# A two-layer decoder trunk in float32: last product with tokens in the rows, coefficient loads on GpSimd's queue, eight buffers for u, and fourteen products on ones at the start

## The chip, the core and the metric

The kernel runs on one core of a Trainium2 chip. The metric is device time in microseconds (us) of one execution, median over runs; lower is better. TensorE is written PE (its weight loads PEld), VectorE DVE, ScalarE ACT, GpSimd POOL, and SyncE SP; SP's and POOL's queues issue DMAs.

## What is computed

The input x has 256 tokens of width 4096. Two layers follow each other; `mem` is a fixed memory of 256 tokens, and every weight is float32.

```
for i in range(2):
    hn   = rmsnorm(h, pre_norm[i])
    u, gate, q, q_gate = split(hn @ w_in[i])            # 3072, 3072, 1024, 1024 wide
    y    = s5_mixer(u, ...) if i == 0 else rglru_mixer(u, ...)
    m    = memory_attention(q, rmsnorm(mem, mem_norm[i]), w_kv[i])
    out  = concat([y * silu(gate), m * silu(q_gate)]) @ w_out[i]     # 4096 wide
    h    = h + rmsnorm(out, post_norm[i])
```

`s5_mixer` is a diagonal state-space recurrence with 192 groups of 16 channels and 64 complex states. Its input coefficients (kept in `Bs` on the chip and in `wD` in DRAM) are a product of `b_re`, `b_im` with powers of a discretised decay that is worked out on the chip.

## The kernel before

Every large product is done in float32 precision from two rounded parts: a raw weight tile of 128 x 1024 (512 KB, tile `raw`) is cast by ACT into `hi`, DVE subtracts to get `lo`, and PE adds hi x hi, hi x lo and lo x hi. One raw tile is one **step**; there are 968 such steps and 12 small ones for the recurrent gates. A step streams 6144 columns through PE in every form. The forms differ in what is held in the array. In "n8", "n2", "n4" and "w2" the weights are held and the activations (`A`, `Bhn`, `Bmix`: features in the rows, 256 tokens along the columns) stream past: "w2" needs 8 products of 512 columns and 8 of 256 a step, the "n" forms 24 of 256. In "v" the activations are held, 128 tokens at a time, and the weights stream: 12 products of 512 columns a step, and the result has tokens in the rows.

The program is written out in one pass by `run`: for each step it places what is due (evacuations, loads, pieces of the side work), then PE's products, then the cast two steps ahead; raw loads are placed four to five steps ahead and go through SP's queue in the order of the program, as all of `dma`'s transfers do. `wraw` has 4 buffers, `whi` and `wlo` 6 halves each (three steps).

The places that matter here:

- **The start.** `setup` sets a tile of ones; the first product of phase "u0" waits for x, its scaled part `A` and the first `hi`.
- **Phase "u0" (24 row blocks).** `ev_u0` multiplies each finished block into a tile `e1` of which there are three, and two steps later sends it to DRAM twice: as `uX` in 64 x 4 x 64 pieces and as `uF`.
- **S5's coefficients.** `s5` is a generator of side work on DVE. It stores the decay as `aD` (three DMAs), later copies `in_s5b3` into `wD`, and then for each half of the groups runs `s5_a_b`: a load step (one DMA of `in_s5bc` and eight of `aD` into `Bs`), three steps of waiting, then multiplications of 128 x 768 on DVE with three pairs of stores `wD<-Bs`. Both halves use the same region of `Bs`. All of it goes through SP's queue. After the stores, `x_load` reads `wD` and `uX` back.
- **The last product (phase "out1").** 128 steps in form "w2" with features in the rows. `ev_out1` squares, scales and keeps each block and loads the residual `h1` beside it; after the last one `rstd` sums the squares over the rows with products on ones, and `final` multiplies and adds in nine pieces (four additions on POOL) and stores them, with features in the rows.

Of the kernel before, what the change touches and what calls it, by code (L numbers as in the profile page):

```python
# [11 lines left out]
F32 = mybir.dt.float32  # L12
# [16 lines left out]
L4 = 4  # L29
TQ = T // L4  # L30
MAGIC = 12582912.0
AHEAD = 8

SM = {}
# [12 lines left out]
def blocks(nm, form=None, n=0):  # L47
    return ([(0, n, form)] if form else []) + [(n, nm - n, "w2")]
# [2 lines left out]
FORMS = {"u0": [(0, 8, "n8"), (8, 4, "n2"), (12, KE - 12, "w2")], "g0": blocks(KE), "gq0": blocks(KX), "q0": blocks(KX),  # L51
         "k0": blocks(KX, "n4", 4), "v0": [(0, KX, "v")], "k1": blocks(KX),
         "glu": blocks(KE, "n4", 4), "out0": blocks(KD), "v1": [(0, KX, "v")],
         "u1": blocks(KE), "gq1": blocks(KX), "q1": blocks(KX), "g1": blocks(KE), "out1": blocks(KD)}


def size(ap):
# [6 lines left out]
class Trunk:  # L64
# [69 lines left out]
    def dma(self, out, in_):  # L134
        out, in_ = (a.bitcast(F32) if a.dtype == F32R else a for a in (out, in_))
        self.nc.sync.dma_start(out=out, in_=in_)  # L136

    def fill(self):
        if self.pieces:
            self.pieces.popleft()()  # L140
# [9 lines left out]
    def setup(self):  # L150
        tc, ctx = self.tc, self.ctx
        P = lambda name, bufs, **kw: ctx.enter_context(tc.tile_pool(name=name, bufs=bufs, **kw))
        self.cpool = P("const", 1)
        self.wraw = P("wraw", 4)
        self.whi = P("whi", 6)
        self.wlo = P("wlo", 6)
        self.big = P("big", 1)
        self.ev = P("ev", 3)
        self.stp = P("st", 2)
        self.ps_acc = P("psacc", 4, space=PSUM)  # L160
        self.ps_x = P("psx", 3, space=PSUM)
# [12 lines left out]
        self.h1 = dt("h1", [KD, 128, T])  # L174
        self.qd = [dt(f"qd{i}", [KX, 128, T]) for i in range(2)]
        self.sq = [dt(f"sqd{i}", [KX, 128, T]) for i in range(2)]
        self.kd = [dt(f"kd{i}", [KX, 128, T]) for i in range(2)]
        self.vd = [dt(f"vd{i}", [2, 128, XA]) for i in range(2)]
        c = self.cpool
        self.sm = c.tile([128, SM_W], F32, name="sm")  # L180
        self.ones = c.tile([128, 128], F32, name="ones")
        self.ident = c.tile([128, 128], F32, name="ident")
        self.n4sp = c.tile([128, KE], F32, name="n4sp")
        self.acc = c.tile([128, 2, T], F32, name="acc")
        self.rbx = c.tile([128, T], F32, name="rbx")
        self.rbm = c.tile([128, T], F32, name="rbm")
        self.colm = c.tile([128, 2], F32, name="colm")
        self.nc.vector.memset(self.ones, 1.0)
        make_identity(self.nc, self.ident)

    def small(self, name, i, n=1):
        o = SM[name][0] + i
# [266 lines left out]

    def ev_u0(self, m, ps):  # L460

        u = self.e("e1")
        v = lambda t: t.rearrange("p (t e) -> p e t", e=L4)
        self.mul(u.rearrange("p (e t) -> p e t", e=L4), v(ps), v(self.rbx))

# [164 lines left out]
            self.put_mixed(self.A, m, g)  # L630
        self.at(self.step + 1, b)

    def ev_out1(self, m, accs, i):
        if m == 0:
            self.fin = self.big.tile([128, 2, KD, T], F32, name="Bfin", tag="B")

        def out(k, ps, g):
            self.act(self.fin[:, 0, k, :], ps, AF.Identity, scale=g)
            self.dma(self.fin[:, 1, k, :], self.h1[k])
        self.ev_out(1, m, accs, i, out, lambda: self.rstd(None, self.colm2, self.step, then=self.final))  # L640

    def final(self):
        k0 = 0
        for c, n in enumerate((4, 4, 4, 4, 4, 4, 4, 2, 2)):
            k = slice(k0, k0 + n)
            k0 += n
            rb = self.pm[:, 0, :].unsqueeze(1).to_broadcast([128, n, T])
            o, h = self.fin[:, 0, k, :], self.fin[:, 1, k, :]
            self.mul(o, o, rb)
            if c in (0, 2, 3, 5):  # L650
                self.nc.gpsimd.tensor_tensor(out=o, in0=o, in1=h, op=ALU.add)  # L651
            else:
                self.add(o, o, h)
            q = self.nc.scalar if c % 2 else self.nc.sync
            q.dma_start(out=self.out[k].rearrange("k p t -> p k t"), in_=o)


    def poly(self, p, x, cs):
# [92 lines left out]
    def s5(self):  # L751
# [43 lines left out]
        self.recip(den, den)  # L795
        yield
        for k, n, rows in ((0, 0, asb[0:NT, 0]), (1, 0, asb[NT:128, 0]), (1, 128 - NT, asb[0:2 * NT - 128, 1])):
            self.dma(self.aD[n:n + rows.shape[0], :, k], rows.rearrange("n (g q) -> n g q", g=2))
        self.mul(t0, nr, lr)
        self.mul(t1, ai, li)  # L800
        self.add(t0, t0, t1)
# [26 lines left out]
        self.mul(t0, nr, den)  # L828
        self.ts(A4[:, :, 0, 1], t0, 2.0, ALU.mult)
        self.ts(A4[:, :, 1, 0], t0, -2.0, ALU.mult)  # L830
        self.dma(self.wD[:, :, L4 - 1].rearrange("t g c x -> t g (c x)"), I["s5b3"].rearrange("t g c x -> t g (c x)"))
        yield
        for h in range(2):
            for f in self.s5_a_b(X0[:, 4096:], h * KE // 2, KE // 2):
                yield f() if f else "wait"
        for _ in range(3):
            yield "wait"
        self.nc.gpsimd.memset(X[:, :, :, 0:1], 0.0)
# [147 lines left out]
    def s5_a_b(self, region, t0, n):  # L986
# [6 lines left out]
        bc = lambda k, h: A[:, h, k].unsqueeze(2).to_broadcast([128, n // 2, 2, 64])  # L993

        def load():
            self.dma(B, self.I["s5bc"][:, tt])
            for g in range(2):
                for i in range(4):
                    r = slice(64 * g + i, 64 * g + 64, 4)
                    self.dma(A[r].rearrange("p t k q -> p t (k q)"),  # L1000
                             a5[i, g, tt].unsqueeze(0).to_broadcast([16, n, 128]))

        def store(e, y):
            for g in range(2):
                r = slice(64 * g, 64 * g + 64)
                self.dma(self.wD[tt, g, e].rearrange("t c (i x) -> (c i) t x", i=4),
                         y[r].rearrange("p t k q -> p t (k q)"))
        work = [load, None, None, None]
        for i, (x, y) in enumerate(((B, P), (P, B), (B, P))):
            def add(h, y=y):  # L1010
                self.sub(y[:, h, 0], y[:, h, 0], Q[:, h, 1])
# [3 lines left out]
                work += [lambda h=h, x=x: self.mul(Q[:, h], x[:, h], bc(1, h)),  # L1015
                         lambda h=h, x=x, y=y: self.mul(y[:, h], x[:, h], bc(0, h)), lambda h=h, add=add: add(h)]
            work.append(lambda i=i, y=y: store(2 - i, y))
        return work

    def seqfill(self):  # L1020
        if self.pieces:
# [212 lines left out]
    def build(self):  # L1234
# [49 lines left out]
        for b in range(12):  # L1284
# [1 line left out]
            self.hook(gates[b] - 12, lambda b=b: self.lru_block(b, self.step + 12))  # L1286
        mark["out1"] = len(self.steps)

        self.add_phase("out1", A, self.ev_out1, ks=list(range(KE, KD)) + list(range(KE)), whole=True,
                       ready=lambda kg: ("att", 1) in self.done)  # L1290


# [67 lines left out]
def layout(i):  # L1360
# [14 lines left out]
    for n, w in W.items():  # L1375
# [5 lines left out]
             "d": cols(A["s5_d"]), "bglu": cols(A["s5_b_glu"]), "cw": cols(A["lru_conv_w"]),  # L1381
             "cb": cols(A["lru_conv_b"]), "ba": cols(A["lru_b_a"]), "bx": cols(A["lru_b_x"]),
             "lam": cols(A["lru_lam"])}
    r["small"] = np.concatenate([parts[n] for n in SM], axis=1)
    pl = lambda v: v.reshape(NT, 128).T
    ls = np.repeat(A["s5_log_step"][0][:, None], 64, axis=1)
# [18 lines left out]
def build_nc(arrays):  # L1405
# [3 lines left out]
    I = {}  # L1409
    for name, a in arrays.items():  # L1410
        I[name] = nc.dram_tensor(f"in_{name}", a.shape, mybir.dt.from_np(a.dtype), kind="ExternalInput").ap()
    out = nc.dram_tensor("out_0", (KD, 128, T), F32, kind="ExternalOutput").ap()
    with tile.TileContext(nc) as tc:
        kernel(tc, I, out)
    return nc
# [10 lines left out]
```

## Time and profile before

| what | us |
|---|---|
| median of 3 runs | 2939.95 (2938.41 to 2943.11) |
| the profiled execution, its own time | 2940.36 |
| its span, first to last instruction | 2938.5 |
| PE busy | 2879.9 (98% of the span) |
| DVE busy / ACT busy / POOL busy | 1994.2 / 1614.4 / 201.1 |
| mean granted clock of PE | 0.994 of 2.4 GHz |

The profiled execution takes 1.9 us more than its span; sums below are made against 2940.36. PE's busy time is modelled from starts, so it counts slow products as busy too: a loss shows either as idle time or as a longer distance from one product to the next.

### The profile page before, as it was taken

The numbers are of one execution on the slowest core, as the hardware profiler recorded it, in microseconds if no ns is written. First come the engines' busy times: TensorE is split into PE (matmuls) and PEld (weight loads), VectorE is DVE, ScalarE is ACT, GpSimd is POOL, SyncE is SP. The second block draws the span as 40 slices with busy tenths as digits, with TensorE's granted clock in tenths as the row PEclk, the third lists the DMA queues.
The fourth block names the chain that finished last, engine by engine and source line by source line (L and its number), as shares of the span: only waits on it lengthen the run. The fifth ranks groups of instructions, "written<-read, shape, count | busy, mean of one in ns | idle before, by whom it ended". The sixth has DMA issues, their size and how long they took to land.

```text
span 2938.5 us, 52696 instructions
## 1 busy us (share of the span) xinstructions
PE 2879.9 (98%) x19182; PEld 2531.3 (86%) x19182; DVE 1994.2 (68%) x3559; ACT 1614.4 (55%) x3042; POOL 201.1 (7%) x223
## 2 busy tenths in 40 slices
PE   8989999999999999999999999999999999999996
PEld 8978888888888898888888888888888888888885
DVE  8776459987695556666555776578888766655555
ACT  6434554445575556566555564466666655555553
POOL 0000000046650000000000110000000000000001
PEclk9999999999999999999999999999999999999998
DMA  8688766676676776676666996666666676666664
GB/s 256 202 257 262 230 198 189 192 218 195 209 217 203 232 242 225 213 242 216 211 199 198 284 293 198 203 207 218 208 217 218 191 225 198 200 203 200 205 202 148
DMA packets 279316, 633.61 MB, mean 216 GB/s; under 512 B 42464, under 2 KB 149216, under 8 KB 279008
## 3 DMA queue, kind: packets, MB, share of 16 engines
q1 hardware_dynamic: 272848, 624.22, 68.2%
q0 software_dynamic: 4352, 4.20, 0.9%
q8 instruction: 150, 2.46, 0.3%
q10 hardware_dynamic: 1856, 1.84, 0.2%
q14 instruction: 110, 0.90, 0.1%
HBM read 585.47 MB, written 46.24 MB: 215 GB/s over the span
## 4 chain that ended last, share of the span: by engine, by line
PE 93%; DVE 3%; DMA 2%; issue 1%; ACT 1%; SPq 0%; DVEq 0%; ACTq 0%
PE acc L132 88%; PE pm L132 2%; PE psg L132 1%; DVE lo L92 1%; PE psx L132 1%; DVE Bs L92 1%; DVE Bfin L92 0%; PE pss L132 0%; PE pso L132 0%; SPq L136 0%; DVE e L92 0%; DMA uF<-e 0%; ACT hi L128 0%; DMA Bs<-in_s5bc 0%; DMA raw<-in_w_u 0%
## 5 line engine op out<-in xcount | busy, mean ns | idle before, releaser
L92 DVE TENSOR_TENSOR lo<-raw,hi 128x512 fp32r<-128x512 f32 x1960 | 1328.3, 699 | 830.0 <-ACT hi L128 812.7
L128 ACT CAST hi<-raw 128x512 fp32r<-128x512 f32 x1960 | 1167.7, 619 | 729.4 <-PE acc L132 607.7
L132 PE MATMUL acc<-A,hi 128*128 128x512 f32 (+1 forms) x4768 | 1478.7, 369 | 9.8 <-ACT A L124 8.0
L132 PE MATMUL acc<-A,lo 128*128 128x256 f32 x4160 | 1168.9, 281 | 17.6 <-DVE lo L92 17.0
L132 PEld LDWEIGHTS acc<-A,hi 128*128 128x128 f32 x4768 | 859.9, 190 | 171.7 <-ACT A L124 8.0
L132 PEld LDWEIGHTS acc<-A,lo 128*128 128x128 f32 x4160 | 788.5, 190 | 24.1 <-DVE lo L92 22.8
L132 PE MATMUL acc<-Bhn,hi 128*128 128x512 f32 x2048 | 719.2, 396 | 2.0 <-ACT hi L128 2.0
L132 PE MATMUL acc<-Bhn,lo 128*128 128x256 f32 x2048 | 572.9, 280 | 1.3 <-DVE lo L92 1.3
L132 PEld LDWEIGHTS acc<-Bhn,hi 128*128 128x128 f32 x2048 | 384.6, 188 | 91.9 <-ACT hi L128 3.1
L132 PEld LDWEIGHTS acc<-Bhn,lo 128*128 128x128 f32 x2048 | 386.6, 189 | 2.8 <-DVE lo L92 2.6
L132 PE MATMUL acc<-Bmix,hi 128*128 128x512 f32 x1024 | 355.0, 394 | 0.0
L132 PE MATMUL acc<-Bmix,lo 128*128 128x256 f32 x1024 | 283.6, 277 | 0.0
L132 PEld LDWEIGHTS acc<-Bmix,hi 128*128 128x128 f32 x1024 | 192.0, 188 | 44.6
L132 PEld LDWEIGHTS acc<-Bmix,lo 128*128 128x128 f32 x1024 | 192.3, 188 | 0.0
L132 PE MATMUL acc<-hi,A 128*128 128x512 f32 x512 | 157.9, 389 | 0.0
L128 ACT COPY e<-acc 128x256 f32<-128x256 f32 x212 | 78.3, 369 | 109.4 <-PE acc L132 108.2
L132 PEld LDWEIGHTS acc<-hi,A 128*128 128x128 f32 x512 | 95.8, 188 | 19.9
L124 ACT ACTIVATE e<-e 128x256 f32<-128x256 f32 x64 | 26.8, 418 | 156.1 <-DVE e L92 155.8
L132 PE MATMUL acc<-lo,A 128*128 128x512 f32 x256 | 99.6, 389 | 0.0
L651 POOL TENSOR_TENSOR Bfin<-Bfin 128x1024 f32<-128x1024 f32 x4 | 10.3, 2588 | 1185.3 <-DVE Bfin L92 1185.3
L92 DVE TENSOR_TENSOR Bs<-Bs 128x256 f32<-128x256 f32 (+3 forms) x131 | 76.3, 586 | 21.8 <-DMA Bs<-aD 21.2
L92 DVE TENSOR_TENSOR e<-e,acc 128x256 f32<-128x256 f32 x212 | 84.5, 411 | 7.1 <-ACT e L128 7.1
(152 smaller groups left out, 1627.9 us busy)
## 6 DMA issues: line engine op xcount, KB each, us to landing
raw<-in_w_out SPq DMA_DIRECT2D x256, 512.0 KB, 4.3
raw<-in_w_u SPq DMA_DIRECT2D x192, 512.0 KB, 4.3
raw<-in_w_g SPq DMA_DIRECT2D x192, 512.0 KB, 4.1
raw<-in_w_glu SPq DMA_DIRECT2D x72, 512.0 KB, 4.3
raw<-in_w_gq SPq DMA_DIRECT2D x64, 512.0 KB, 4.4
raw<-in_w_q SPq DMA_DIRECT2D x64, 512.0 KB, 4.3
raw<-in_w_k SPq DMA_DIRECT2D x64, 512.0 KB, 4.5
raw<-in_w_v SPq DMA_DIRECT2D x64, 512.0 KB, 4.6
```

Source lines behind the costliest of these rows:

```text
L92: self.nc.vector.tensor_tensor(out=out, in0=a, in1=b, op=op)
L124: self.nc.scalar.activation(out=out, in_=a, func=f, **kw)
L128: self.nc.scalar.copy(out=out, in_=a)
L132: self.nc.tensor.matmul(out, lhsT=lhsT, rhs=rhs, start=start, stop=stop)
L651: self.nc.gpsimd.tensor_tensor(out=o, in0=o, in1=h, op=ALU.add)
```

## The change

The phase "out1" takes form "v": 128 tokens are held at a time and the weights stream, so the result has tokens in the rows. Its scale (`post_norm`) is read as rows from a new input `postr`, squares are summed along the free axis by ACT, and `final` turns the residual with PE transposes, scales and adds in 16 pieces on DVE, and stores each. Four kinds of DMA of `s5` (aD, in_s5bc, in_s5b3, wD) go from SP's queue to POOL's by `gdma`; the loads of both halves are issued at once, ahead of most of the decay's powers, into two regions, and the three steps of waiting stand once. `ev_u0` rotates through tags e1, e2, e3 with 3, 3 and 2 buffers. Fourteen products of ones by ones stand at PE's head. The output array and its host layout change to tokens in rows.

```diff
+NWARM = 14
...
-         "u1": blocks(KE), "gq1": blocks(KX), "q1": blocks(KX), "g1": blocks(KE), "out1": blocks(KD)}
+         "u1": blocks(KE), "gq1": blocks(KX), "q1": blocks(KX), "g1": blocks(KE), "out1": [(0, KD, "v")]}
...
+    def gdma(self, out, in_):
+
+        self.nc.gpsimd.dma_start(out=out, in_=in_)
...
+        for _ in range(NWARM):
+            self.nc.tensor.matmul(self.pm[:, 0, 0:128], lhsT=self.ones, rhs=self.ones, start=True, stop=True)
...
     def ev_u0(self, m, ps):
 
-        u = self.e("e1")
+        u = self.ev.tile([128, T], F32, name="u", tag=f"e{m % 3 + 1}", bufs=(3, 3, 2)[m % 3])
...
-    def ev_out1(self, m, accs, i):
...
+    def out1_load(self, g):
+
+        if g == 0:
+            fin = self.big.tile([128, 4, 2048 * 2], F32, name="Bfin", tag="B")
+            self.fo = fin[:, 0:2]
+            self.fh = fin[:, 2:4].rearrange("p a (k t) -> p (a k) t", t=T)
+            self.ssq = self.stp.tile([128, 2, 8], F32, name="nv", tag="nv", bufs=2)
+        self.gain = self.stp.tile([128, 2, T], F32, name="st", tag="st").rearrange("p a b -> p (a b)")
+        self.dma(self.gain, self.I["postr"][g].unsqueeze(0).to_broadcast([128, 512]))
+        for k in range(4 * g, 4 * g + 4):
+            self.dma(self.fh[:, k], self.h1[k])
+
+    def ev_out1(self, g, n, ps):
+        self.mul(self.fo[:, n, 512 * g:512 * g + 512], ps, self.gain)
+        sq = self.stp.tile([128, 2, T], F32, name="sq", tag="sq", bufs=1).rearrange("p a b -> p (a b)")
+        self.act(sq, ps, AF.Square, accum_out=self.ssq[:, n, g:g + 1])
+        if g == 7 and n == 1:
+            self.final()
 
     def final(self):
-        k0 = 0
...
+        pieces = [(n, g) for g in range(8) for n in range(2)]
+        ps = {}
+
+        def turn(i):
+            if i >= len(pieces):
+                return
+            n, g = pieces[i]
+            ps[i] = (self.ps_x if i % 7 < 3 else self.ps_acc).tile([128, 2, T], F32, name="pst" if i % 7 < 3 else "acc",
+                                                                 tag="x" if i % 7 < 3 else "acc")
+            p = ps[i].rearrange("p a b -> p (a b)")
+            for k in range(4):
+                self.nc.tensor.transpose(p[:, 128 * k:128 * k + 128], self.fh[:, 4 * g + k, n * 128:n * 128 + 128],
+                                         self.ident)
+        for i in range(7):
+            turn(i)
+        v = self.stp.tile([128, 2, 8], F32, name="nv", tag="nv", bufs=2).rearrange("p a b -> p (a b)")
+        self.nc.vector.tensor_reduce(out=v[:, 8:10], in_=self.ssq, axis=mybir.AxisListType.X, op=ALU.add)
...
+        for i, (n, g) in enumerate(pieces):
+            o = self.fo[:, n, 512 * g:512 * g + 512]
+            self.stt(o, o, v[:, 4 + n:5 + n], ps.pop(i).rearrange("p a b -> p (a b)"), ALU.mult, ALU.add)
+            q = self.nc.scalar if i % 2 else self.nc.sync
+            q.dma_start(out=self.out[n, :, 512 * g:512 * g + 512], in_=o)
+            turn(i + 7)
...
         for k, n, rows in ((0, 0, asb[0:NT, 0]), (1, 0, asb[NT:128, 0]), (1, 128 - NT, asb[0:2 * NT - 128, 1])):
-            self.dma(self.aD[n:n + rows.shape[0], :, k], rows.rearrange("n (g q) -> n g q", g=2))
+            self.gdma(self.aD[n:n + rows.shape[0], :, k], rows.rearrange("n (g q) -> n g q", g=2))
+        ab = [self.s5_a_b(X0[:, 4096 + 6144 * h:], h * KE // 2, KE // 2) for h in range(2)]
+        for load, _ in ab:
+            load()
...
-        self.dma(self.wD[:, :, L4 - 1].rearrange("t g c x -> t g (c x)"), I["s5b3"].rearrange("t g c x -> t g (c x)"))
-        yield
-        for h in range(2):
-            for f in self.s5_a_b(X0[:, 4096:], h * KE // 2, KE // 2):
-                yield f() if f else "wait"
+        self.gdma(self.wD[:, :, L4 - 1].rearrange("t g c x -> t g (c x)"), I["s5b3"].rearrange("t g c x -> t g (c x)"))
+        yield
+        for _ in range(3):
+            yield "wait"
+        for _, work in ab:
+            for f in work:
+                yield f()
...
-        self.add_phase("out1", A, self.ev_out1, ks=list(range(KE, KD)) + list(range(KE)), whole=True,
+        for g in range(8):
+            self.hook(mark["out1"] + 4 + 16 * g, lambda g=g: self.out1_load(g))
+        self.add_phase("out1", A, self.ev_out1, ks=list(range(KE, KD)) + list(range(KE)),
```

The first place is SP's queue in phase "u0", where the coefficients of the first half are loaded (`raw` is a weight tile, `e_...` and `u` are finished blocks of u, `Bs_370` is the region of the coefficients). Before:

```order
L136 DMA raw<-in_w_u 128x1024
L136 DMA wD<-in_s5b 48x8192
L136 DMA raw<-in_w_u 128x1024
L136 DMA uX<-e_1883 64x4x64 x2
L136 DMA uF<-e_1883 128x256
L136 DMA uX<-e_1885 64x4x64 x2
L136 DMA uF<-e_1885 128x256
L136 DMA Bs_370<-in_s5bc 128x1536
L136 DMA Bs_370<-aD 16x12x128 x8
L136 DMA raw<-in_w_u 128x1024 x6
```

The same place in the changed program:

```order
L137 DMA raw<-in_w_u 128x1024 x2
L137 DMA uX<-u 64x4x64 x2
L137 DMA uF<-u 128x256
L137 DMA uX<-u 64x4x64 x2
L137 DMA uF<-u 128x256
L137 DMA raw<-in_w_u 128x1024 x8
```

The ten coefficient DMAs no longer stand between two raw loads. They stand on POOL's queue, which had none of them (there, row `MEMSET` followed `AFFINE_SELECT` at once); in the changed program POOL's queue begins, behind the identity matrix, with:

```order
L141 DMA aD<-Bs_384 192x1x64
L141 DMA aD<-Bs_384 64x1x64
L141 DMA aD<-Bs_384 128x1x64
L141 DMA Bs_384<-in_s5bc 128x1536
L141 DMA Bs_384<-aD 16x12x128 x8
L141 DMA Bs_384<-in_s5bc 128x1536
L141 DMA Bs_384<-aD 16x12x128 x8
L141 DMA wD<-in_s5b 48x8192
L141 DMA wD<-Bs_384 64x12x128 x12
L879 MEMSET Bs_384 128x192
```

All 34 DMAs of the coefficients stand one behind the other, and the loads of both halves stand ahead of the copy of `in_s5b3` and of every store.

The second place is PE's end, behind the last product. Before (`A` is the mixed activation, `pm` the sums over the rows):

```order
L132 MATMUL acc<-A,lo 128x256
L132 MATMUL acc<-A,hi 128x512
L132 MATMUL acc<-A,lo 128x256
L132 MATMUL pm<-ones,acc 128x1 x4
L132 MATMUL pm<-dg,ones 128x128 x2
```

In the changed program (`Bfin` here is the residual, `pst` and `acc` are the PSUM tiles that take its transposes):

```order
L133 MATMUL acc<-hi,A 128x512 x2
L133 MATMUL acc<-lo,A 128x512
L673 MATMUL pst<-ident,Bfin 128x128 x12
L673 MATMUL acc<-ident,Bfin 128x128 x16
L673 MATMUL pst<-ident,Bfin 128x128 x12
L673 MATMUL acc<-ident,Bfin 128x128 x16
L673 MATMUL pst<-ident,Bfin 128x128 x8
```

The six products of the norm are gone from PE's end, and 64 transposes of the residual stand there.

## Rows read from the trace of the kernel before

**Rows 1.** The page, busy time: engine, us (share), instructions.

```profile
PE 2879.9 (98%) x19182; PEld 2531.3 (86%) x19182; DVE 1994.2 (68%) x3559; ACT 1614.4 (55%) x3042; POOL 201.1 (7%) x223
```

**Rows 2.** Table by stretch: busy us, PE's clock, DMA share, GB/s.

```profile
104.00:141.00 37.00, 34.40 (x277) 33.27 (x276) 27.93 (x77) 14.33 (x25) 0.00 (x0) 1.00 0.70 198
141.00:165.60 24.60, 15.40 (x118) 15.20 (x117) 10.44 (x17) 5.47 (x10) 0.00 (x0) 0.86 0.79 261
205.20:212.90 7.70, 4.64 (x19) 3.74 (x18) 7.27 (x11) 2.90 (x5) 0.00 (x0) 0.78 0.86 282
212.90:260.00 47.10, 47.10 (x268) 40.83 (x268) 38.34 (x62) 21.68 (x37) 2.22 (x3) 1.00 0.97 291
104.00:260.00 156.00, 141.13 (x899) 127.41 (x898) 114.49 (x214) 60.44 (x103) 2.22 (x3) 0.97 0.86 258
2910.80:2938.50 27.70, 2.42 (x14) 1.89 (x12) 20.21 (x24) 2.00 (x5) 10.28 (x4) 0.59 0.46 151
```

**Rows 3.** Timeline of the start: start, length, instruction, [idle before <-releaser].

```profile
0.84 0.17 DVE L188 MEMSET ones<- 128x128 f32 x1 [0.84 <-PEq L1408]
...
7.99 1.10 PE L132 MATMUL acc<-A,hi 128*128 128x256 f32 x2 [7.99 <-ACT A L124]
...
13.58 0.63 PE L132 MATMUL acc<-A,hi 128*128 128x256 f32 x2
...
14.22 0.45 PE L132 MATMUL acc<-A,hi 128*128 128x256 f32 x2
...
15.34 0.40 PE L132 MATMUL acc<-A,hi 128*128 128x256 f32 x2
...
15.70 0.40 PE L132 MATMUL acc<-A,hi 128*128 128x256 f32 x2
```

**Rows 4.** Waits of DVE and PE, 100 to 215 us: total, times, longest.

```profile
DVE e L92 <- DMA uF<-e: 7.7, 4, 5.4
...
PE acc L132 <- DVE lo L92: 14.1, 5, 9.2
```

**Rows 5.** Timeline of DVE where it waits for the coefficients of a half.

```profile
158.53 2.42 DVE L92 TENSOR_TENSOR Bs<-Bs 128x768 f32<-128x768 f32 x3 [13.74 <-DMA Bs<-aD]
...
205.56 2.42 DVE L92 TENSOR_TENSOR Bs<-Bs 128x768 f32<-128x768 f32 x3 [7.44 <-DMA Bs<-aD]
```

**Rows 6.** Timeline of SP's queue, where the first half's coefficients are loaded.

```profile
149.70 5.12 SPq L136 DMA_DIRECT2D Bs<-aD  x8
154.91 13.14 SPq L136 DMA_DIRECT2D raw<-in_w_u  x6
```

**Rows 7.** Timeline of ACT: the copy that the `aD` stores read.

```profile
108.79 0.41 ACT L128 COPY Bs<-psa 128x128 f32<-128x128 f32 x2
```

**Rows 8.** DMA issues: xcount, KB each, median us to landing.

```profile
bh<-in_x POOLq DMA_DIRECT2D x16, 256.0 KB, 7.3
```

**Rows 9.** POOL's one kind of DMA, line 580: ns min/median/max.

```profile
L580 POOL DMA_DIRECT2D bh<-in_x x16: 1194/1203/1332, 1633.8 to 1734.6; - x16
```

**Rows 10.** The chain that ended last, from the last product on: start, us.

```profile
2481.07 429.88 PE acc L132 x2480
...
2914.33 0.17 DVE nv L112
...
2916.09 1.23 PE pm L132 x4
2917.35 2.36 DVE Bfin L92 x2
...
2934.47 0.69 DVE Bfin L92
```

**Rows 11.** Timeline of PE in phase "v1", form "v".

```profile
1759.59 0.62 PE L132 MATMUL acc<-hi,A 128*128 128x512 f32 x2
...
1764.35 0.62 PE L132 MATMUL acc<-hi,A 128*128 128x512 f32 x2
```

**Rows 12.** PE's transposes in the attention: ns min/median/max.

```profile
L1084 PE MATMUL pst<-ident,p x32: 270/272/274, 1075.7 to 2470.6; 128*128 128x128 f32 x32
```

More of the change, by code (lines that the diff above doesn't have):

```diff
@@ L631, in ev_g1 @@
         self.at(self.step + 1, b)
-    def ev_out1(self, m, accs, i):
[L634 to L640, printed above, removed]
-    def final(self):
-        k0 = 0
[L644 to L655, printed above, removed]
+    def out1_load(self, g):
[8 more added lines that the diff above has]
+            self.dma(self.fh[:, k], self.h1[k])
@@ new lines, in ev_out1 @@
+    def ev_out1(self, g, n, ps):
[4 more added lines that the diff above has]
+            self.final()
+    def final(self):
+        pieces = [(n, g) for g in range(8) for n in range(2)]
[14 more added lines that the diff above has]
+        self.nc.vector.tensor_reduce(out=v[:, 8:10], in_=self.ssq, axis=mybir.AxisListType.X, op=ALU.add)
+        self.ts(v[:, 0:2], v[:, 8:10], 1.0 / D, ALU.mult, EPS, ALU.add)
+        self.act(v[:, 2:4], v[:, 0:2], AF.Sqrt)
+        self.recip(v[:, 4:6], v[:, 2:4])
+        self.mul(v[:, 6:8], v[:, 4:6], v[:, 4:6])
+        self.mul(v[:, 6:8], v[:, 6:8], v[:, 0:2])
+        self.ts(v[:, 6:8], v[:, 6:8], -0.5, ALU.mult, 1.5, ALU.add)
+        self.mul(v[:, 4:6], v[:, 4:6], v[:, 6:8])
+        for i, (n, g) in enumerate(pieces):
[4 more added lines that the diff above has]
+            turn(i + 7)
@@ L995, in load @@
         def load():
-            self.dma(B, self.I["s5bc"][:, tt])
+            self.gdma(B, self.I["s5bc"][:, tt])
             for g in range(2):
@@ L999, in load @@
                     r = slice(64 * g + i, 64 * g + 64, 4)
-                    self.dma(A[r].rearrange("p t k q -> p t (k q)"),
+                    self.gdma(A[r].rearrange("p t k q -> p t (k q)"),
                              a5[i, g, tt].unsqueeze(0).to_broadcast([16, n, 128]))
@@ L1005, in store @@
                 r = slice(64 * g, 64 * g + 64)
-                self.dma(self.wD[tt, g, e].rearrange("t c (i x) -> (c i) t x", i=4),
+                self.gdma(self.wD[tt, g, e].rearrange("t c (i x) -> (c i) t x", i=4),
                          y[r].rearrange("p t k q -> p t (k q)"))
-        work = [load, None, None, None]
+        work = []
         for i, (x, y) in enumerate(((B, P), (P, B), (B, P))):
@@ L1017, in s5_a_b @@
             work.append(lambda i=i, y=y: store(2 - i, y))
-        return work
+        return load, work
     def seqfill(self):
@@ L1383, in layout @@
              "lam": cols(A["lru_lam"])}
+    r["postr"] = np.ascontiguousarray(A["post_norm"][1].reshape(8, 512))
     r["small"] = np.concatenate([parts[n] for n in SM], axis=1)
@@ L1411, in build_nc @@
         I[name] = nc.dram_tensor(f"in_{name}", a.shape, mybir.dt.from_np(a.dtype), kind="ExternalInput").ap()
[L1412 removed]
+    out = nc.dram_tensor("out_0", (2, 128, D), F32, kind="ExternalOutput").ap()
     with tile.TileContext(nc) as tc:
@@ L1424 @@
     o = np.asarray(r.results[0]["out_0"])
-    return np.ascontiguousarray(o.reshape(D, T).T).reshape(1, T, D)
+    return np.ascontiguousarray(o.reshape(1, T, D))
```

## Prediction

> **What bounds the kernel.** I read the busy times first: PE is busy 98% of the span [rows 1]. But a busy PE can be a slow one, so the next view is the distance from one product to the next, stretch by stretch. In the last product 2480 products take 429.88 us, 0.1733 each, 2.773 us for a step of 16 [rows 10]; nothing waits there, PE alone sets the time. The losses are at four other places. At the start the first product begins at 7.99 us, and three products of 256 columns take 0.64 us (13.58 to 14.22) until 14.22 and 0.36 after it (15.34 to 15.70): the lower level of the clock, then the upper [rows 3]. From 100 to 215 us PE waits 14.1 us for `lo` tiles of DVE, and DVE waits 7.7 us for the stores of `uF` that keep a u tile occupied [rows 4] and 13.74 and 7.44 us for `aD` loads [rows 5]. What stands behind the waiting instruction in DVE's order are the `lo` tiles of the next steps. At the end nothing but 27.7 us of evacuation, norm and stores is left, with PE busy for 2.4 of it [rows 2]. The stretch between 260 us and the last product is left as it is.
>
> **Products on ones.** Fourteen are added, behind a tile of ones that is written by 1.01 us [rows 3]. Two such products (four instructions) take 1.23 us at the lower level with their latency [rows 10], so fourteen take at most 8.6 us and would end at 9.6, and about half at the upper level, 4.3. So they end between 5.3 and 9.6; back to back, where the latency is paid once, I estimate 7: in time for the first product. If the clock is up by then, the 6.23 us from 7.99 to 14.22 shrink from 9.7 triples of 0.64 to 9.7 of 0.36, 3.5 us: 2.7 gained. If they end at 9.6, 1.6 of that is lost; if the clock is not up, nothing is gained. I take 2.0, nearer the upper end, because 7 us is longer than the 6.23 us after which the clock rose in this trace. The Trainium skill ("TensorE: Matmul & The Clock Gate", Part 1) says that the throttled clock is the default, that activity lifts it, and that the moment does not hang on the kernel's own start but varies from run to run. The trace agrees on the first two (0.64, then 0.36 a triple); one execution cannot show the third, by which this term could be anything from 0 to 2.7.
>
> **u's buffers and the coefficient loads.** What PE lost is taken by pitch. A product of 256 columns costs 0.12 (0.36/3) at the upper level; from 104 to 141 us, 277 of them need 33.2 us and took 37.0: 3.8 lost. From 141 to 165.6, 118 need 14.2 of 24.6: 10.4 lost, one wait of DVE for `aD` and the clock's fall behind it (0.86 granted). From 205.2 to 212.9, 19 products at 0.176 (47.10/268, the next stretch) need 3.3 of 7.7: 4.4 lost to the second half's load and a granted 0.78 [rows 2]. Together 18.6.
>
> With eight tiles instead of three, u's products no longer wait for the stores. With the loads on POOL, SP does not spend 5.12 us on eight of them ahead of six raw loads [rows 6]. Each costs POOL 1.2 us [rows 9], and POOL has nothing else to do there. Are they in time? The copy that `aD` is stored from ends at 109.2 [rows 7]. Three stores (3.6), their landing, nine loads (10.8) and a landing follow: 29 us with the 7.3 that POOL's loads take to land [rows 8]; the second half needs 11 more. DVE stood ready for the first half at 144.8 (158.53 less 13.74 [rows 5]) and will be, with the 3.8 us gained ahead of it, at 141: 31.8 us after the copy. So it fits with 3 us to spare. The second half is asked for a half's work later: from 158.5 to 198.1 (205.56 less 7.44) less three waiting steps of 2.83 (16 products of 0.176), 31 us; it fits with 23 to spare. What hides the whole cost is POOL's idleness and this distance; if it were gone, each late microsecond beyond PE's lead of about two steps (5.5 us) is lost.
>
> What is late next are the raw loads themselves. From 104 to 260 us the DMA engines are used to 0.86 at 258 GB/s, 40.2 MB; 18.6 us less would be 293 GB/s at 0.98. The densest stretch, 212.9 to 260, ran at 291 and 0.97 with no idle PE; the one before it reached 282 [rows 2]. 40.2 MB at 291 leave 0.8 us of the loss standing, at 282 they leave 5.2. The loads now also bunch in the part where u's small pieces are written, so I take 4 back. The step: 18.6 - 4 = 14.6.
>
> **The last product.** Form "v" streams the same columns in 12 products instead of 16. In phase "v1" 21 products take 4.76 us (1759.59 to 1764.35), 2.72 a step of 12 [rows 11]. 128 steps of 2.773 - 2.720 save 6.8 us. Its evacuation (two multiplications on DVE and two squares on ACT per 16 steps) is less than that of before, and DVE and ACT have more than half a step free; "v1" shows the pitch with its evacuation, so I take no other cost.
>
> **The end.** Before, the end takes 27.7 us [rows 2]. Now, behind the last product: one multiplication and one square, which I put at 1.4; a small reduction, 0.2; then the small operations of the norm, 1.5 of the 1.76 between 2914.33 and 2916.09. The copies, additions and the six products go. So the first of 16 pieces starts at 3.1 us. A piece of 512 columns costs DVE between 0.59 (half of 2.36/2) and 0.69 [rows 10]: the last ends at 12.5 to 14.1, and with the 3.3 us that lay behind DVE's last operation before (2935.2 to 2938.5) the end is at 15.8 to 17.4. But the output is 4.19 MB; at 291 GB/s [rows 2] its stores take 14.4 us behind the first piece (3.7), 18.1, and a little for the last landing. The transposes, 64 at no more than 0.27 [rows 12], take at most 17.3, with the last piece and its store 21.3. I take 18.8, the stores: 27.7 - 18.8 = 8.9 saved, between 6.4 and 11.9.
>
> **Sum.** 2.0 + 14.6 + 6.8 + 8.9 = 32.3. The profiled execution took 2940.4 us, 0.4 above the median of the runs; 2940.4 - 32.3 = 2908.
>
> **Rivals.**
> First: the transfers are the bound, and moving them only moves the wait. For it speaks the share of 0.97 to 0.98 that the sum above needs, against it that PE did not idle once at 0.97 [rows 2]. Then DVE or ACT wait for `aD` or raw tiles about as long as now, and of the change 2.0 + 6.8 + 8.9 = 17.7 are left: 2922.7. The Trainium skill ("DMA: Bandwidth & Descriptors", Issuing engines are not separate DMA queues) speaks for this rival: whichever engine issues, the same 16 DMA engines do the work, and only the time to issue is saved. By that rule alone the edit saves SP's 5.12 us twice and no more. The trace shows the sharing only as far as raw loads and coefficients lie in one queue there.
>
> Second, the other side: slower. POOL makes its transfers slowly where they are cut small. A `wD` store has 64 x 12 = 768 runs, the `bh` loads of 1.2 us have 256; by runs a store would cost 3.6 us. A pair's tile is written again one multiplication later, some 10 us (a third of the 31 us of a half's work), and the first load back from `wD` stands on SP ahead of raw loads. Two stores and a landing of 7.3 must fit in that and PE's lead of 5.5: up to about 4.4 us a store nothing is lost; beyond it 6 us per microsecond of store (two of a pair, at two rewritings and one load back). The 32 gained elsewhere are gone, and 6 more, at about 11 us a store, three times the price by runs: 2946 or more.
>
> Third: the end is not shortened. If the transposes, at the lower clock that the end shows (0.59 [rows 2]), do not keep ahead of DVE, or stores of 2 KB rows go slower, 8.9 is lost: 2917. Against it: seven pieces are turned before the first is needed.
>
> **Chances and range.** Forecast 0.62; the first rival 0.18, the third 0.10, the second 0.05; 0.05 for smaller mixtures of the first and the second, 2924 to 2940. Likeliest alone: 2901 to 2914. The range goes from 2897 (start 2.7, nothing taken back, the end at 15.8) to 2924, with the first and the third rival in it. 0.2% (5.9 us) is about what a measurement of this kernel tells from no change: faster 0.92, same 0.03, slower 0.05.
>
> **What would show it.** Start: 0.36 a triple from the first product. u and coefficients: no wait of DVE for `uF`; none for `aD`, and PE idle under 4 us from 104 to 260, with a granted clock of 1.00; raw loads with nothing between them in SP's queue. Last product: 2.72 a step. End: 16 pieces on DVE at 0.6 to 0.7 and stores that reach 290 GB/s. Wrong would be the sum if DVE waits for a load from POOL, if SP's first read of `wD` holds raw loads, or if PE's transposes come late at the end.

## The result, and the profile after

The changed kernel takes 2906.64 us (median of 4 runs, 2902.31 to 2908.03); the kernel before took 2940.09 beside it (2938.41 to 2943.11). The ratio is 0.9886, with a 95% interval of 0.9874 to 0.9897: 33.5 us faster. The profiled execution took 2907.16 with a span of 2905.4, so its span is 33.1 shorter. The forecast was 2908, in a range of 2897 to 2924.

The page's busy times (engine, us, share, instructions) show no more than that the same work is done in less time:

```profile
PE 2880.1 (99%) x18750; PEld 2517.1 (87%) x18750; DVE 1980.9 (68%) x3528; ACT 1596.1 (55%) x2994; POOL 212.3 (7%) x253
```

The table by stretch of the changed kernel (busy us of PE, PEld, DVE, ACT, POOL with their instructions, then PE's clock, the DMA share and GB/s), stretches of [rows 2], then the end, and one about the late raw loads:

```profile
104.00:141.00 37.00, 34.33 (x282) 33.69 (x281) 25.82 (x70) 12.13 (x22) 12.31 (x22) 1.00 0.98 303
141.00:165.60 24.60, 24.60 (x162) 23.00 (x162) 23.03 (x37) 11.91 (x20) 1.56 (x2) 0.93 0.88 285
205.20:212.90 7.70, 7.70 (x46) 6.66 (x45) 7.38 (x12) 3.11 (x5) 0.00 (x0) 1.00 0.94 314
104.00:260.00 156.00, 153.32 (x1051) 138.26 (x1050) 119.71 (x220) 69.18 (x120) 23.60 (x37) 0.99 0.88 278
2887.60:2905.40 17.80, 9.12 (x65) 6.75 (x63) 12.67 (x25) 1.58 (x5) 0.00 (x0) 0.84 0.64 236
110.00:145.00 35.00, 32.33 (x253) 31.69 (x253) 23.03 (x62) 11.82 (x21) 9.77 (x18) 0.96 1.04 327
```

Against [rows 2] the two holes at 141 and at 205 us are closed, and PE idles 2.7 us between 104 and 260 instead of 14.9. What is left lies ahead of 141 us, with a granted clock of 0.93 in the stretch behind it; there the DMA engines are now full: 327 GB/s at a share of 1.04 from 110 to 145 us. The waits from 100 to 215 us (total, times, longest) say who is late there:

```profile
ACT hi L129 <- DMA raw<-in_w_u: 21.4, 8, 4.7
...
PE acc L133 <- ACT hi L129: 2.8, 2, 2.2
...
PE acc L133 <- DVE lo L93: 0.4, 2, 0.2
```

DVE waits neither for `uF` nor for `aD` any more (7.7 and 21.2 us before [rows 4, 5]), PE hardly for `lo` (14.1 before). What PE now waits for is `hi`, which ACT makes from raw tiles that come late. ACT had waited for raw tiles before, and no less:

```profile
ACT hi L128 <- DMA raw<-in_w_u: 26.1, 7, 8.9
```

Now it is the wait that reaches PE.

Where the 33.1 us come from, by the two traces. A step is counted by its 6144 columns; the times are the starts of PE's first product of a step, and the last product's end is the start of its last two steps and 5.55 or 5.44 us.

| stretch | before | after | gained | forecast |
|---|---|---|---|---|
| start to step 2 | 16.78 | 13.76 | 3.0 | 2.0 |
| step 2 to step 80 | 245.30 | 231.57 | 13.7 | 14.6 |
| step 80 to step 838 | 2288.17 | 2288.54 | -0.4 | 0 |
| step 838 to the end of the last product | 360.53 | 353.73 | 6.8 | 6.8 |
| end | 27.7 | 17.8 | 9.9 | 8.9 |

The start (timeline of PE: start, length, instruction, [idle before <-releaser]):

```profile
1.06 5.43 PE L196 MATMUL pm<-ones 128*128 128x128 f32 x28 [1.06 <-DVE ones L193]
7.23 0.38 PE L133 MATMUL acc<-A,hi 128*128 128x256 f32 x1 [0.74 <-ACT A L125]
...
13.40 0.40 PE L133 MATMUL acc<-A,hi 128*128 128x256 f32 x2
...
13.76 0.40 PE L133 MATMUL acc<-A,hi 128*128 128x256 f32 x2
```

The fourteen products end at 6.49, and the triples take 0.36 us from the first one on. The first product also began 0.76 sooner, because x's tiles landed sooner in this execution. It begins at 6.6 to 8.0 us in four executions without the products on ones and at 6.5 to 7.7 in eight with them, so I take that for scatter.

POOL's queue (timeline of the transfers it issues):

```profile
106.34 1.95 POOL L141 DMA_DIRECT2D aD<-Bs  x3 [105.02 <-ACT Bs L129]
108.16 0.72 POOL L141 DMA_DIRECT2D Bs<-in_s5bc  x1
112.99 4.35 POOL L141 DMA_DIRECT2D Bs<-aD  x8 [4.11 <-DMA aD<-Bs]
119.39 0.57 POOL L141 DMA_DIRECT2D Bs<-in_s5bc  x1 [2.05 <-DMA Bs<-aD]
...
129.72 0.54 POOL L141 DMA_DIRECT2D wD<-in_s5b  x1
154.18 1.56 POOL L141 DMA_DIRECT2D wD<-Bs  x2 [23.92 <-DVE Bs L93]
```

A load of `aD` costs POOL 0.54 us, a store of `wD` with its 768 runs 0.78, both less than the 1.2 of [rows 9]. Between the first half's loads and the last one POOL also waits 7.5 us, by this trace for earlier loads to land; why it has to isn't shown. The last load is issued at 129.7; DVE begins the first half's work at 145.3 without a wait.

The end (timeline of DVE and of the queues that store; three pieces and the last two):

```profile
2887.12 1.38 DVE L93 TENSOR_TENSOR Bfin<-acc,st 128x512 f32<-128x512 f32 x2 [6.36 <-PE acc L133]
...
2891.02 2.06 DVE L106 SCALAR_TENSOR_TENSOR Bfin<-Bfin,nv,pst 128x512 f32<-128x512 f32 x3
2891.79 9.55 SPq L690 DMA_DIRECT2D out<-Bfin  x8
...
2892.45 9.56 ACTq L690 DMA_DIRECT2D out<-Bfin  x8
...
2900.24 1.40 DVE L106 SCALAR_TENSOR_TENSOR Bfin<-Bfin,nv,pst 128x512 f32<-128x512 f32 x2
```

The 16 pieces lie on DVE without a gap, from 2891.02 to 2901.64, 0.66 each. The DMA view from 2888 us on shows the stores beside them (share in tenths and GB/s in 40 slices of 0.435 us; then the issues and their landing):

```profile
DMA  0000000000399999999999999999999999990000
GB/s 0 0 0 0 0 0 0 0 0 0 122 372 367 377 372 386 391 367 391 381 381 391 381 377 386 377 372 395 372 381 381 377 391 381 377 381 14 0 0 0
...
out<-Bfin SPq DMA_DIRECT2D x8, 256.0 KB, 2.3
out<-Bfin ACTq DMA_DIRECT2D x8, 256.0 KB, 2.3
```

DVE delivers 256 KB per 0.66 us, 395 GB/s; the engines move about 380 and are full. The two are level, and neither leaves the other much to wait for.

### The profile page after: what moved, and what is told of

Same layout as the page of the kernel before. It is cut to its first block, busy times and chain, and to the rows that moved or that the text cites. A ratio compares the mean times of both kernels' runs of the same rounds, so it can differ in the third digit from the quotient of the medians.

```text
span 2905.4 us, 51774 instructions
## 1 busy us (share of the span) xinstructions
PE 2880.1 (99%) x18750; PEld 2517.1 (87%) x18750; DVE 1980.9 (68%) x3528; ACT 1596.1 (55%) x2994; POOL 212.3 (7%) x253
## 4 chain that ended last, share of the span: by engine, by line
PE 94%; DVE 3%; DMA 1%; issue 1%; ACT 1%; DVEq 0%; SPq 0%; ACTq 0%
PE acc L133 89%; PE pm L133 1%; PE psg L133 1%; DVE lo L93 1%; PE psx L133 1%; DMA raw<-in_w_u 1%; DVE Bs L93 1%; PE pss L133 0%; PE pso L133 0%; ACT hi L129 0%; DVE Bfin L106 0%; DVE e L93 0%; PE psd L133 0%; DMA st<-in_mem 0%; DVE A L106 0%
## 5 line engine op out<-in xcount | busy, mean ns | idle before, releaser
L133 PE MATMUL acc<-A,hi 128*128 128x512 f32 (+1 forms) x3744 | 1120.6, 362 | 5.0 <-ACT hi L129 3.9
L133 PE MATMUL acc<-A,lo 128*128 128x256 f32 x3136 | 882.6, 281 | 4.2 <-DVE lo L93 4.0
L133 PEld LDWEIGHTS acc<-A,hi 128*128 128x128 f32 x3744 | 666.5, 190 | 122.4 <-ACT hi L129 5.4
L133 PEld LDWEIGHTS acc<-A,lo 128*128 128x128 f32 x3136 | 594.9, 190 | 9.3 <-DVE lo L93 8.4
L133 PE MATMUL acc<-hi,A 128*128 128x512 f32 x1536 | 473.0, 389 | 0.0
L133 PEld LDWEIGHTS acc<-hi,A 128*128 128x128 f32 x1536 | 288.0, 188 | 59.4
L133 PE MATMUL acc<-lo,A 128*128 128x512 f32 x768 | 298.8, 389 | 0.0
L133 PEld LDWEIGHTS acc<-lo,A 128*128 128x128 f32 x768 | 144.2, 188 | 30.1
L129 ACT COPY e<-acc 128x256 f32<-128x256 f32 x180 | 66.5, 369 | 75.5 <-PE acc L133 74.0
L587 POOL DMA_DIRECT2D bh<-in_x x16 | 19.4, 1210 | 840.1 <-ACT hi L129 800.7
```

The source lines that it names most:

```text
L129: self.nc.scalar.copy(out=out, in_=a)
L133: self.nc.tensor.matmul(out, lhsT=lhsT, rhs=rhs, start=start, stop=stop)
L587: self.nc.gpsimd.dma_start(out=h, in_=self.I["x"][2 * c:2 * c + 2].rearrange("k p t -> p k t"), accum_op=ALU.add)
```

## The experiments

My theory after the result: the 13.7 us between steps 2 and 80 come from three things that need each other (a queue of POOL's own, an early place, eight buffers), and what is still lost there is lost to full DMA engines. The rivals: one of the three did it all and the rest is idle; or what is left is lost to SP's order or to DVE. The losses below are those of step 2 to step 80 in the profiled execution, above the 226.49 us of spread2, the lowest.

| run | u's tiles | coefficients | step 2 to 80, lost us | ratio to before [95%] |
|---|---|---|---|---|
| before | 3 | SP, late | 18.8 | 1 |
| changed | 8 | POOL, early | 5.1 | 0.9886 [0.9874, 0.9897] |
| after2, the same again | 8 | POOL, early | 1.9 | 0.9888 [0.9874, 0.9901] |
| u8_only | 8 | SP, late | 12.8 | 0.9973 [0.9964, 0.9983] |
| pool_late | 3 | POOL, one region | 21.0 | 1.0013 [1.0004, 1.0022] |
| u3 | 3 | POOL, early | 14.0 | 0.9926 [0.9912, 0.9939] |
| sp_early | 8 | SP, early | 10.8 | 0.9920 [0.9907, 0.9934] |
| double_copy | 8 | POOL, early, 1.57 MB more | 9.0 | 0.9898 [0.9884, 0.9911] |
| spread | 8 | POOL, 3.1 MB from 1.49 us on | 0.0 | 0.9907 [0.9894, 0.9921] |
| spread2 | 8 | POOL, 3.1 MB earlier, from 52 us on | 0 | 0.9876 [0.9862, 0.9889] |
| spread2_u3 | 3 | as spread2 | 7.6 | 0.9897 [0.9882, 0.9912] |

u8_only, pool_late, warm_only and tail_only are the kernel before with one thing added, so they lack the gains of the start or the end; the others are the changed kernel with one or two things altered. A loss is read from one execution: warm_only and tail_only, in this stretch the kernel before, lose 18.5 and 16.9, and the changed kernel's two executions differ by 3.2. So a difference of some 3 us between two rows says nothing.

**The changed kernel once more** (after2, no edit).

> The changed kernel once more, beside the others on their chip: ratio 0.9886 within 0.001 (2907 where the kernel before takes 2940). If the start is at the mercy of when the first tiles of x land, step 2 stands somewhere between 13 and 14 us instead of exactly at 13.76.

2907.04 against 2939.05, ratio 0.9888. Step 2 stood at 12.99 us. The loss between steps 2 and 80 was 1.9 here and 5.1 in the first trace: it varies from one execution to the next.

**Eight buffers alone** (u8_only, on the kernel before).

```diff
-        u = self.e("e1")
+        u = self.ev.tile([128, T], F32, name="u", tag=f"e{m % 3 + 1}", bufs=(3, 3, 2)[m % 3])
```

> The kernel before with u's eight buffers alone. By my sum the buffers are worth the 3.8 us lost between 104 and 141 us, if SP's queue then reaches the loads of aD as much sooner: about 3.5 less than the kernel before, DVE without a wait for uF and with the same 13.7 and 7.4 for aD. Rival, that the time regained is lost again in a longer wait for aD: no change, within 1.5, with a wait of 17 us for aD. By the run u3 the buffers are worth 9 where the coefficient loads lie beside u's stores; if they are worth 9 here too, both are wrong.

2931.49 against 2939.63: 8.1 less (5.0 to 10.6 by the interval), more than 3.5, and not nothing. DVE's waits from 100 to 215 us:

```profile
DVE Bs L92 <- DMA Bs<-aD: 19.9, 2, 13.2
```

The wait for `uF` is gone and the one for `aD` is as it was (21.2 in [rows 5]): the time regained isn't lost there again. The trace gives 6.0 us between steps 2 and 80: the 3.8 of the forecast, and most of the rest at the second half's load, where PE idles 2.2 instead of 3.1 us and the granted clock from 196 to 210 us stays at 1.00 (0.78 from 205 to 213 before [rows 2]).

**The queue alone** (pool_late, on the kernel before; the new method `gdma` issues on POOL).

```diff
-            self.dma(self.aD[n:n + rows.shape[0], :, k], rows.rearrange("n (g q) -> n g q", g=2))
+            self.gdma(self.aD[n:n + rows.shape[0], :, k], rows.rearrange("n (g q) -> n g q", g=2))
...
-            self.dma(B, self.I["s5bc"][:, tt])
+            self.gdma(B, self.I["s5bc"][:, tt])
```

(and so for the loads of `aD`, the copy of `in_s5b3` and the stores of `wD`)

> The kernel before with its four kinds of coefficient transfers on GpSimd's queue, at their old late places and with one region. Theory that the place matters: DVE asks for a half's coefficients when it wants them, so it still waits about 13 and 7 us for aD (9 loads at 0.6 us and a landing of 7.4), and PE behind it; only the raw loads gain: 2935 to 2940. Rival, that what cost was SP's queue held by nine loads: most of the 14 us of those two places are gained, about 2926.

2940.84 against 2937.35: nothing gained, and by the interval 1.2 to 6.5 lost. The rival's 2926 is out, but the first theory's 2935 to 2940 is missed too, and its mechanism isn't what the trace shows. POOL's queue issued the first half's loads at 109.85 us, though they are written later in the program, since nothing that waits stands between the decay's stores and them on that engine; only the second half's came late, at 188 us. DVE's waits from 100 to 215 us:

```profile
DVE e L92 <- DMA uF<-e: 17.0, 4, 14.0
DVE Bs L92 <- DMA Bs<-aD: 10.7, 1, 10.7
```

One wait for `aD` remains, and the other has become a wait for `uF`: u's stores now run beside the copy and the loads and land later (13.3 us for the two `uF` stores issued from 107 to 113 us, where the kernel before has a median of 3.5 from 105 to 145), and three tiles aren't enough. This run with eight buffers wasn't made, so the early place and the second region are not told apart from each other; both together, at three buffers, are worth 7.0 us by the traces (21.0 here, 14.0 in u3).

**Three buffers in the changed kernel** (u3).

```diff
-        u = self.ev.tile([128, T], F32, name="u", tag=f"e{m % 3 + 1}", bufs=(3, 3, 2)[m % 3])
+        u = self.e("e1")
```

> The changed kernel with u in three buffers, as before. Theory that the eight buffers matter: the stores of u take longer than before between 110 and 145 us, because the coefficient loads lie beside them (uX 5.4 us to landing against 4.1), so DVE waits for them again and by more than the 7.7 us of before: 3 to 8 us more than the changed kernel. Rival, that the raw loads bind there anyway and the buffers are worth nothing: within 1.5 us of the changed kernel.

2916.09 against 2907.04 of the changed kernel on the same chip: 9 more, a little over the theory's 8. The expectation's 5.4 and 4.1 us are medians of whole executions; from 105 to 145 us `uX` takes 7.4 us to land in the changed kernel and 3.7 in the one before. DVE's wait for `uF` (total, times, longest):

```profile
DVE e L93 <- DMA uF<-e: 18.4, 4, 7.1
```

**Early, but on SP's queue** (sp_early).

```diff
     def gdma(self, out, in_):
 
-        self.nc.gpsimd.dma_start(out=out, in_=in_)
+        self.nc.sync.dma_start(out=out, in_=in_)
```

> The changed kernel with all coefficient transfers back on SP's queue, but placed early as in the change. Theory that the queue matters: the loads of aD wait for the aD stores to land (4.1 us on GpSimd's queue) and 18 loads at about 0.64 us follow, 15.6 us in which no raw load is issued; PE's lead of two steps (5.7 us) covers a part, and of the rest some 5 are lost now too: 5 to 10 us more than the changed kernel, 2912 to 2917, with ACT waiting for raw tiles. Rival, that the gain is the early placement alone and the queue is worth nothing: 2906.6 within 2.

2913.9, ratio 0.9920 where the changed kernel has 0.9886 to 0.9888: 9 to 10 us more, so the queue is worth something of its own. SP's queue in that run:

```profile
114.26 5.12 SPq L141 DMA_DIRECT2D Bs<-aD  x8
119.42 0.59 SPq L141 DMA_DIRECT2D Bs<-in_s5bc  x1
120.06 5.71 SPq L141 DMA_DIRECT2D Bs<-aD  x8
125.87 0.56 SPq L137 DMA_DIRECT2D raw<-in_w_u  x1
```

Its last raw load ahead of these was issued at 106.2 us; ACT waits up to 14.6 us for a raw tile, and PE idles 7.17 us from 124.99 on. Between steps 2 and 80 it loses 10.8, u8_only with the late place on the same queue 12.8: on SP's queue the early place is worth nothing that can be told.

**Three megabytes moved ahead** (spread, on the changed kernel).

```diff
         yield from self.exp_gen(dt, th, tmp[0:4] + [ki])
+        ab = [self.s5_a_b(X0[:, 4096 + 6144 * h:], h * KE // 2, KE // 2) for h in range(2)]
+        self.gdma(self.wD[:, :, L4 - 1].rearrange("t g c x -> t g (c x)"), I["s5b3"].rearrange("t g c x -> t g (c x)"))
...
+        self.gdma(B, self.I["s5bc"][:, tt])
+
         def load():
-            self.gdma(B, self.I["s5bc"][:, tt])
```

(the later `ab =` and copy are taken out)

> The changed kernel with three of its transfers on GpSimd's queue earlier: both loads of in_s5bc and the copy of in_s5b3 stand ahead of the decay's computation instead of behind the aD stores. My theory: the 5.0 us that PE loses at steps 43 to 45 (2.96 + 1.79 + 0.28 above 2.88 a step, with the clock's fall behind them) come from full DMA engines between 110 and 145 us (share 1.04, 327 GB/s); the 3.1 MB moved go where the share is 0.70 (20 to 104 us), so the loss goes: 2906.6 - 5.0 = about 2901.6, share of that stretch under 0.95. Rival one: it is u's small stores ahead of the raw loads in SP's queue, or DVE's work, that make the raw loads late: no change, 2906.6 within 1.5. Rival two: the moved transfers now take from the raw loads earlier: 2907 or more, with new waits between 20 and 104 us.

2909.14, ratio 0.9907 where the changed kernel has 0.9886: some 6 us slower by the ratios, whose intervals still touch, and 2 between the two profiled spans. My theory and the second rival were each half right. From 110 to 145 us PE no longer idles (35.00 busy of 35). But POOL, which waits for nothing there, issued the three transfers from 1.49 us on, among the first raw tiles, and the second step stood without weights:

```profile
1.49 1.27 POOL L141 DMA_DIRECT2D Bs<-in_s5bc  x2 [0.17 <-issue]
...
15.86 1.14 ACT L129 CAST hi<-raw 128x512 fp32r<-128x512 f32 x2 [4.17 <-DMA raw<-in_w_u]
...
16.52 0.67 PE L133 MATMUL acc<-A,hi 128*128 128x256 f32 x2 [2.48 <-ACT hi L129]
```

Step 2 began at 21.24 us, 7.5 later than in the changed kernel, with a granted clock of 0.67 from 10 to 20 us.

**The same, held back to 50 us** (spread2, on spread).

```diff
+        self.nc.gpsimd.tensor_copy(out=X0[:, 5632:5633], in_=dt[:, 0:1])
         ab = [self.s5_a_b(X0[:, 4096 + 6144 * h:], h * KE // 2, KE // 2) for h in range(2)]
```

> As the run spread, but GpSimd's three early transfers wait for a number that DVE writes at about 50 us, so that they don't lie in the first 20 us (in spread they were issued at 1.49 us, and step 2 came 7.5 us later). Theory of full DMA engines: the 5.0 us at steps 43 to 45 are gone as in spread, and the start is as in the changed kernel: 5.0 less than the changed kernel on the same chip, ratio about 0.987. Rival, that three megabytes cost PE the same wherever they lie: no less than the changed kernel, ratio 0.9886.

2902.86 against 2907.04 of the changed kernel on the same chip, 4.2 less; but the intervals of the two ratios overlap, and the profiled executions of the two have the same span, 2900.6 (the changed kernel's lost 1.9 in this stretch and began step 2 at 12.99 us, this one at 13.98). So a gain in time isn't shown. That the loss is gone, the table by stretch shows:

```profile
110.00:145.00 35.00, 35.00 (x294) 35.00 (x293) 26.15 (x67) 13.31 (x23) 8.66 (x16) 1.00 0.96 270
104.00:260.00 156.00, 156.00 (x1105) 141.04 (x1105) 120.29 (x221) 70.66 (x123) 21.79 (x34) 1.00 0.86 266
```

PE doesn't idle at all from 104 to 260 us, and the clock is never lower. Its median is the lowest of all.

**One copy twice** (double_copy, on the changed kernel).

```diff
+        self.gdma(self.wD[:, :, L4 - 1].rearrange("t g c x -> t g (c x)"), I["s5b3"].rearrange("t g c x -> t g (c x)"))
         for load, _ in ab:
             load()
```

> The changed kernel with the copy of in_s5b3 (1.57 MB) made twice, the added one ahead of the coefficient loads at 106 us. Theory of full DMA engines: 1.57 MB at the 290 to 327 GB/s of that stretch is 4.8 to 5.4 us more, all of it lost by PE: about 2912 where the changed kernel takes 2907. Rival, that the raw loads are late there for another reason (SP's order, u's stores): within 1.5 us of the changed kernel.

2909.71, ratio 0.9898: about 3 more than the changed kernel, with intervals that overlap, so the medians alone don't show it. The trace does: 9.0 lost between steps 2 and 80 against 5.1 and 1.9, so 3.9 to 7.1 more, with PE idle for 5.5 us from 110 to 145 us:

```profile
110.00:145.00 35.00, 29.45 (x224) 28.34 (x223) 20.10 (x56) 8.80 (x15) 9.76 (x18) 0.95 1.02 323
```

The place and the trace's size are the theory's; the median's size is short of it, and the rival's 1.5 is not excluded by the medians.

**Three buffers with the moved transfers** (spread2_u3: spread2 with the edit of u3).

> The run spread2 with u in three buffers again. Theory that the buffers matter because u's stores are slow beside full DMA engines: with three megabytes taken out of that stretch DVE waits less for uF than the 18.4 us of u3, and the buffers are worth 3 to 5 us instead of 9: 2906 to 2908 where spread2 takes 2903. Rival, that three buffers are too few for u's stores at any load of the engines: 9 again, 2912.

2910.30, ratio 0.9897 against 0.9876: some 6 to 7 more than spread2 (7.6 between steps 2 and 80), between the two forecasts; the intervals overlap here too. DVE waits less than the 18.4 us of u3:

```profile
DVE e L93 <- DMA uF<-e: 12.0, 4, 6.4
```

So full engines make a part of the wait, and three tiles are too few for the rest.

**The fourteen products alone** (warm_only, on the kernel before).

```diff
+        for _ in range(NWARM):
+            self.nc.tensor.matmul(self.pm[:, 0, 0:128], lhsT=self.ones, rhs=self.ones, start=True, stop=True)
```

> The kernel before with only the fourteen products of ones by ones added at PE's head. By the two traces PE stands 3.0 us further ahead from step 2 on in the changed kernel (0.76 of it because the first product began earlier, 7.23 against 7.99): between 2.3 and 3.0 gained, 2937.1 to 2937.8, with 0.36 us a triple from the first product. Rival: the clock rises at a moment of its own and the one changed execution that was profiled had luck: 0 gained in the median, 2940.

2936.12 against 2937.35, ratio 0.9994 (0.9985 to 1.0003): 1.2 us, between the two, and not to be told from nothing. The traces say why. Without the products, the triples went from 0.64 to 0.36 us at 14.22 (before [rows 3]), at 11.22 (pool_late), at 11.21 (u8_only) and at 10.56 (tail_only). PE in pool_late and its first product:

```profile
6.63 0.58 PE L132 MATMUL acc<-A,hi 128*128 128x256 f32 x1 [6.63 <-ACT A L124]
...
11.22 0.49 PE L132 MATMUL acc<-A,hi 128*128 128x256 f32 x2
```

That is 6.2, 4.6, 3.5 and 3.0 us after the first product. So step 2 begins anywhere from 14.90 to 16.78 without the products (four traces), and from 12.98 to 13.98 with them (eight, spread left out): a gain of 0.9 to 3.8, 2.2 by the means (15.5 and 13.3). Of these 2.2 the first product's earlier start makes 0.5; counted from the first product, step 2 comes after 8.0 us without and 6.4 with the products, 1.6 gained.

**The last product and the end alone** (tail_only: the kernel before with the form "v", `out1_load`, `ev_out1` and `final` of the change).

> The kernel before with the last product, its evacuation and the end of the change alone. Theory of separate terms: the two traces give 6.8 for the product and 9.9 for the end (27.7 to 17.8), 16.7 together: 2940.1 less 16.7, 2923.4, ratio 0.9943. Rival, that a part of it came from what the change moved elsewhere (the order of the last phase, transfers into it): less than 13 gained, ratio above 0.9955.

2918.29 against 2939.05, ratio 0.9931 (0.9918 to 0.9943): 16.8 to 24.1 by the interval, 20.8 by the medians. Its five runs lie 9.7 us apart. Its trace has 6.8 less in the last product, and an end of 18.9 us behind it:

```profile
2899.70:2918.60 18.90, 9.17 (x65) 6.74 (x63) 12.72 (x25) 1.58 (x5) 0.00 (x0) 0.83 0.60 223
```

So 15.6 are the two terms'; the other 4.3 of the 19.9 between the spans lie ahead of the last product, at the start (1.8), between steps 2 and 80 (1.9) and behind them (0.5), where it reads as the kernel before. I take them for scatter; that isn't shown. The end is steadier: 17.6 to 17.8 us in the eight other profiled executions with the new end, 27.7 to 27.9 in the four with the old one.

## Why the prediction was right, point by point

**Products on ones.** Right by the traces, and the size about so: 2.0 forecast, 3.0 in the pair of profiles (0.76 of it x's landing), 1.6 by the means of many traces, counted from the first product. Alone, in the medians, it can't be told from nothing (1.2, between -0.9 and 4.4). The products took 5.43 us, in the bounds of 4.3 to 8.6. The sentence of the Trainium skill that the prediction weighed ("TensorE: Matmul & The Clock Gate", Part 1: the moment at which the clock rises is not tied to the kernel's start and differs from run to run) is now borne out by rows: 6.2, 4.6, 3.5 and 3.0 us after the first product.

**u's buffers and the coefficient loads.** The sum was right, 13.7 against 14.6, and so was the reason for taking something back, full engines: 5.1 and 1.9 are lost in two profiles, and the runs with 1.57 MB more and with 3.1 MB moved shift this loss to 9.0 and to 0. That the 4 fits is in part luck: the prediction's own rates allowed 0.8 to 5.2. Three steps inside were not right; the sum survived them because it took the whole 18.6 as removable, however it was split. First, POOL's price of 1.2 us a transfer, from [rows 9], was too high: 0.54 for a load of `aD` and 0.78 for a store. The `bh` transfers of [rows 9] are of another kind, they add to what the tile holds (`accum_op` in line 580), and the coefficients are only copied; whether that makes the price isn't shown. So the first half's loads were issued by 117.3 and, with a landing of 7.4, lay ready 20 us before DVE took them up at 145.3, not 3. Second, the buffers were put at 3.8, what is lost ahead of 141 us; that was too low. Alone they are worth 8.1 (6.0 in the trace), and 9 within the change: with the loads beside u's stores and three tiles, DVE waits 18.4 us for `uF`. The prediction added parts that don't add: the queue alone gave nothing (1.0013) because the wait moved to u's tiles. Third, it did not see that POOL's queue brings the first half's loads early by itself, wherever they are written (109.85 in pool_late); by that trace the new place and the second region matter for the second half, whose loads came at 188 us there. So the theory of three things that need each other is right in part: against the three executions of the kernel before in this stretch, eight buffers alone gain 4.1 to 6.0, POOL's queue and the early place with three buffers 2.9 to 4.8 (u3), and all together 11.8 to 16.9, more than the two added.

The first rival, that the transfers bind, is what holds the last 2 to 5 us, at 1.04 from 110 to 145 us, no more. The Trainium skill ("DMA: Bandwidth & Descriptors", Issuing engines are not separate DMA queues) says that transfers run on the same 16 DMA engines whichever engine starts them, and that starting them from several saves issue time alone. The trace agrees on the first: with POOL's loads beside SP's the share is 1.04 and the raw tiles are late. On the second the prediction counted 5.12 us twice; the second half's eight loads had held SP for 7.80 (from 194.30). And sp_early is 9 to 10 us slower with the same bytes: in one queue a raw load also waits until all that stands ahead of it has been issued, with its waits (no raw load was issued from 106.2 to 125.87 us).

**The second rival**, slow stores on POOL, is out: two stores of 768 runs take 1.56 us, not 7.2, and no wait for them is seen.

**The last product.** 6.8 forecast; 6.8 measured, in the changed kernel and in tail_only (2.72 us a step in both).

**The end.** 9.9 measured against 8.9 forecast. The mis-sized step is the stores' rate: 291 GB/s, taken from a mixed stretch, would have held the end to 18.8. The stores ran at about 380, and so DVE's 16 pieces of 0.66 (forecast 0.59 to 0.69), level with the engines, set 17.8. The first piece came at 3.4 us after the last product, 3.1 forecast; the transposes kept ahead, against the third rival.

## What to carry to other kernels

When a wait is taken away, ask which buffer the same stretch fills next: here the loads on their own queue and the tiles for u were worth nothing and 8 us alone, and 14 together with the early place and the second region. A transfer that waits for nothing starts when its queue reaches it, not where it stands in the program; tie it to a number that is made at the time when the engines have room. A rate for stores at the end is read from a stretch of the same kind, not from one in which other transfers mix.

## What the runs showed of the hardware

POOL's price per transfer didn't follow the number of runs: 1.2 us for the `bh` loads of 256 runs, which add to the tile, 0.54 for a load of `aD` with 192 and 0.75 to 0.78 for a store of 768. The stores of the output, in rows of 2 KB from two queues, ran at 367 to 395 GB/s with the engines full; the loads at the start of spread ran at 400 at a share of 1.00, but the stretch from 110 to 145 us, in which u's small pieces are written beside the loads, at 327 with a share of 1.04. Full engines are not one rate.
